# Seven products of quarters for two feature groups instead of one, with three of the four sums of weights made by accumulating DMAs

## The chip, the cores and the metric

The kernel runs on one core of one Trainium2 chip. The metric is device time in microseconds (us). The kernel before took 2288.77 us (median of three runs, 2286.74 to 2290.21).

## The reference

Two transformer layers over 256 tokens of width 2048, in float32. Each layer is a mixer (a gated delta rule with a linear recurrence in the first, two kinds of attention in the second) followed by a gated feed-forward network (FFN) of width 5632. The change touches the two FFNs alone, so only they matter here:

```python
def swiglu(hn, w_gate, w_up, w_down):
    return (jax.nn.silu(hn @ w_gate) * (hn @ w_up)) @ w_down
...
        h = h + swiglu(rmsnorm(h, ffn_norm[layer]), ffn_w_gate[layer], ffn_w_up[layer], ffn_w_down[layer])
```

`hn` is 256 x 2048, `w_gate` and `w_up` are 2048 x 5632, `w_down` is 5632 x 2048.

## The kernel before

**Numbers in two parts.** A float32 operand is split into `hi`, its value rounded to TensorE's fp32r format, and `lo`, the rest. A product is hi·hi + hi·lo + lo·hi, three matmuls. For the weights, ScalarE (ACT) makes `hi` by a copy and VectorE (DVE) makes `lo` by a subtraction: `split`, lines 174 and 175. A load is always a 128 x 1024 tile of 512 KB (`load`, line 168, issued from SyncE's queue, SP). It holds two feature tiles of 128 for 512 output columns, and is called a unit below. `load` rotates over three buffers of `raw`, and in the FFNs every fourth load goes to the extra buffer `raw4`; the hi and lo tiles have four and three buffers (`whi`, `wlo`).

**A block.** `block` computes two products of 512 columns at once (`i` = 0 and 1): gate and up in the first half of an FFN, two column groups of the down projection in the second. The tokens are in two halves of 128 (`t`). Four PSUM banks `F[t][i]` collect the results. The features are in groups `m` of 512, that is four feature tiles, or two units for each `i`. A gate/up block has four groups. The 5632 hidden features are handled in pieces of 4, 4 and 3 groups: a piece makes as many gate/up blocks as it has groups, then two down blocks over those groups. An FFN has 11 gate/up blocks, four down blocks with four groups and two with three.

**A plain group** costs four units. Each unit is multiplied with both token halves: 2 feature tiles x 2 halves x 3 matmuls = 12 matmuls, 48 for the group (`Bank.add`, lines 366 to 368).

**A group by seven products.** Group 0 of each block is treated as a 2 x 2 matrix product of quarters: activations by token half and feature half, weights by feature half and `i` (b11, b12, b21, b22, one unit each). In place of eight quarter products of six matmuls there are seven, 42 matmuls, over sums and differences of quarters. Four combinations of the activation quarters are made once per FFN or piece by `combine` and kept in `comb`. The weights need four sums per block, made by `total` (lines 337, 340, 341): DVE adds two tiles into `T`, ACT copies `T` to `thi`, DVE subtracts to `tlo`. The sums are T1 = b11+b12, T3 = b12+b22, T2 = T1+b22, T4 = T2+b21. Products go to four more banks `M`, or straight into `F`; `ends` (lines 413 to 415) combines the `M` banks into the tiles `e`, which the end of a block adds to `F`.

**Order.** `seven` is a generator that yields after each of its seven products; `block` runs through the plain units `j` and takes steps of `seven` between them. A planner then orders the instructions of each engine. Engines run their own queues in order and wait on each other by semaphores. At the end of a gate/up block DVE adds `F` and `e` into `fa` (L472, L476, L477) and ACT takes the silu (L473); the block after it transposes `fa` into `hid` on TensorE between its plain units (`turn`, L453). At the end of a down block DVE adds `e` and then `F` into `h` (L488, L491).

Of the kernel before, what the change touches and what calls it, by code (L numbers as in the profile page):

```python
# [6 lines left out]
ALU = mybir.AluOpType  # L7
# [4 lines left out]
T = 256  # L12
# [35 lines left out]
def body(tc, A, out):  # L48
# [129 lines left out]
    def unit(src):  # L178

        return split(load(src))  # L180
# [96 lines left out]

    def sumsq(g, *ts):
        for t in ts or range(2):
            j = mx.tile([128, 512], F32, name="junk", tag="t2", bufs=4)  # L280
            S.activation(j, h[:, t, g * 512:(g + 1) * 512], AF.Square, accum_out=ssp[:, t, g:g + 1])

    def to_x(g, w, late=False):
# [47 lines left out]
        return f  # L331


    def total(a, b, name):

        t = mx.tile([128, 1024], F32, name=name, tag="T", bufs=3)
        V.tensor_tensor(out=t, in0=a, in1=b, op=ALU.add)
        hi = mx.tile([128, 1024], F32R, name="thi", tag="thi", bufs=2)
        lo = mx.tile([128, 1024], F32R, name="tlo", tag="tlo", bufs=2)
        S.copy(hi, t)  # L340
        V.tensor_sub(lo, t, hi.bitcast(F32))  # L341
        return t, (hi, lo)

    def combine(x4):

        f = mx.tile([128, 4, T], F32, name="cf", tag="cf", bufs=1)
        c = mx.tile([128, 4, 2, 128], F32, name="cc4", tag="cc4", bufs=1)
        r = mx.tile([128, 2, 4, 2, 128], F32R, name="comb", tag="comb", bufs=2)
        V.tensor_tensor(out=f, in0=x4[:, :, 0].bitcast(F32), in1=x4[:, :, 1].bitcast(F32), op=ALU.add)
        a11, a21, a12, a22 = (f[:, 2 * j:2 * j + 2, t * 128:(t + 1) * 128] for j in range(2) for t in range(2))  # L350
        for i, (x, y) in enumerate(((a21, a22), (a21, a11), (a22, c[:, 1]), (a12, c[:, 2]))):
            V.tensor_tensor(out=c[:, i], in0=x, in1=y, op=ALU.subtract)
# [18 lines left out]
    def block(src, x, comb, nd, hooks, tail=0):  # L371
# [38 lines left out]

        def ends():
# [3 lines left out]
                V.tensor_tensor(out=o, in0=a.t, in1=b, op=op)  # L415
            return [[c1, w5], [v, w7]]

        sevens = [s for m in comb for s in [seven(m)] for _ in range(7)]
        lead, trail = 2, 3 if nd > 3 else 2
        gaps = max(len(plain) - lead - trail, 1)  # L420
        held, e, k = [], None, 0
        for j, (i, u) in enumerate(plain):
            if j in hooks:
                hooks[j]()
            w = unit(src(i, u))
            held.append((i, u, w))
            if j < len(plain) - tail:
                todo, held = [(*held[0], (0, 1))], []
            elif j < len(plain) - 1:
                continue  # L430
            else:
                todo = [(*y, (t,)) for t in range(2) for y in held]
            for i1, u1, w1, tt in todo:
                for t in tt:
                    F[t][i1].add(lambda kk: xs(2 * u1 + kk, t), w1)
            tick()
            while k < len(sevens) and k < (j - lead + 2) * len(sevens) // gaps:
                next(sevens[k])
                k += 1
                if k == len(sevens):  # L440
                    e = ends()
        return [[y.t for y in f] for f in F], e

    def ffn(L, then, fin=None):
# [14 lines left out]
        for piece in (4, 4, 3):  # L459
            hid = ogp.tile([128, 16, 2, T], F32R, name="hid", tag="hid")  # L460
            for j in range(piece):
                hooks = {2: turn, 3: turn} if todo else {}
                if b == 0:
                    hooks[1] = lambda: cx.update({0: combine(X[:, 0:4])})
                    hooks[8] = rstd
                if j == 1:
                    hooks[5] = lambda: ch.update({0: combine(hid[:, 0:4])})
                F, e = block(lambda i, u: gu[b, u, i], lambda k: X[:, k], {0: lambda: cx[0]}, 4, hooks)
                a = [mx.tile([128, 512], F32, name=f"fa{t}", tag="fa", bufs=4) for t in range(2)]
                for t in range(2):  # L470
                    r = nrm["rs"][:, t:t + 1]
                    V.tensor_tensor(out=a[t], in0=F[t][0], in1=e[t][0], op=(ALU.add, ALU.subtract)[t])  # L472
# [698 lines left out]
```

## Time and profile before

| | |
|---|---|
| median of the runs | 2288.77 us (2286.74 to 2290.21) |
| the profiled execution's own time | 2286.04 us |
| its span, first to last instruction | 2284.2 us |
| granted TensorE clock over the span | 0.996 |
| busy share: TensorE (PE), DVE, ACT, GpSimd (POOL) | 99%, 79%, 53%, 0% |
| DMA | 422.35 MB, 185 GB/s on average |

The profile lists busy time by engine, a chain of work followed back from the last instruction, groups of instructions by line with their mean duration, and DMA issues with the time from issue to landing. Matmuls overlap in the records, so their cost is the distance from one start to the next and not the listed duration. The same holds, by about a tenth of a microsecond, for DVE and ACT. A few per cent of the records can be missing.

### The profile page before, as it was taken

The page shows a single profiled execution, that of the slowest core. Times are in us where ns is not written, and L with a number is a line of the kernel's source. Part 1 is how long each engine was busy: PE and PEld are TensorE (multiplying, and loading weights), DVE is VectorE, ACT ScalarE, POOL GpSimd, SP SyncE. Part 2 cuts the span into 40 slices and gives each one's busy share as a digit, 9 for nine tenths or more (in the row PEclk, how much of TensorE's full clock was granted, in tenths as well). Part 3 has the DMA queues.
Part 4 walks back from the last instruction along what each step waited for, and adds up shares of the span by engine and source line. Part 5 has one row for each costly group of instructions (what it writes and reads, how often), then busy time and mean ns, then how long its engine had stood idle before and what let it go on. Part 6 is the DMA issues. An engine that isn't in the chain of part 4 may idle for free.

```text
span 2284.2 us, 31143 instructions
## 1 busy us (share of the span) xinstructions
PE 2259.0 (99%) x11620; PEld 1906.7 (83%) x11620; DVE 1805.0 (79%) x2655; ACT 1205.9 (53%) x1580; POOL 2.0 (0%) x6
## 2 busy tenths in 40 slices
PE   8999999999999999999999999999999999999997
PEld 8999888788888888888878888887888888888886
DVE  6898676688887888888976658857888788787888
ACT  6765654554554554454654444445554455554554
POOL 0000000000000000000000000000000000000000
PEclk9999999999999999999999999999999999999999
DMA  7444445566565566566554455455565565566564
GB/s 244 148 161 155 145 154 181 167 203 201 185 204 202 188 208 192 191 200 201 185 169 166 151 172 168 166 191 179 186 208 194 192 205 197 183 206 204 186 213 147
DMA packets 118647, 422.35 MB, mean 185 GB/s; under 512 B 13248, under 2 KB 14784, under 8 KB 118368
## 3 DMA queue, kind: packets, MB, share of 16 engines
q1 hardware_dynamic: 118208, 419.84, 55.4%
q8 instruction: 91, 1.49, 0.3%
q10 hardware_dynamic: 288, 0.52, 0.1%
q14 instruction: 60, 0.49, 0.1%
HBM read 418.22 MB, written 2.10 MB: 184 GB/s over the span
## 4 chain that ended last, share of the span: by engine, by line
PE 97%; DVE 1%; DMA 1%; ACT 1%; issue 0%; DVEq 0%; ACTq 0%; SPq 0%
PE F L366 17%; PE F L368 17%; PE F L367 17%; PE Pw L194 7%; PE Pw L199 6%; PE Px L268 5%; PE Px L270 4%; PE Px L269 4%; PE M L367 3%; PE M L368 3%; PE M L366 3%; PE Pw L197 2%; PE Pw L198 2%; PE Ph L453 1%; PE Psc L975 1%; DVE wlo L175 0%
## 5 line engine op out<-in xcount | busy, mean ns | idle before, releaser
L174 ACT CAST whi<-raw 128x1024 fp32r<-128x1024 f32 x744 | 779.9, 1052 | 889.1 <-PE F L368 424.1
L175 DVE TENSOR_TENSOR wlo<-raw,whi 128x1024 fp32r<-128x1024 f32 x744 | 906.1, 1222 | 329.5 <-PE F L367 141.9
L366 PE MATMUL F<-whi,X 128*128 128x512 f32 x1100 | 432.2, 393 | 5.6 <-ACT whi L174 5.6
L368 PE MATMUL F<-whi,X 128*128 128x512 f32 x1100 | 429.6, 391 | 0.0
L367 PE MATMUL F<-wlo,X 128*128 128x512 f32 x1100 | 429.4, 390 | 0.0
L199 PE MATMUL Pw<-X,wlo 128*128 128x256 f32 x1104 | 310.2, 281 | 0.0
L366 PEld LDWEIGHTS F<-whi,X 128*128 128x128 f32 x1100 | 206.8, 188 | 48.7 <-ACT whi L174 7.1
L368 PEld LDWEIGHTS F<-whi,X 128*128 128x128 f32 x1100 | 207.2, 188 | 43.6
L367 PEld LDWEIGHTS F<-wlo,X 128*128 128x128 f32 x1100 | 207.5, 189 | 42.1
L194 PE MATMUL Pw<-X,whi 128*128 128x512 f32 x640 | 230.2, 403 | 0.0
L366 PE MATMUL F<-whi,hid 128*128 128x512 f32 x536 | 209.9, 392 | 0.0
L199 PEld LDWEIGHTS Pw<-X,wlo 128*128 128x128 f32 x1104 | 209.5, 190 | 0.2
L368 PE MATMUL F<-whi,hid 128*128 128x512 f32 x536 | 208.7, 389 | 0.0
L367 PE MATMUL F<-wlo,hid 128*128 128x512 f32 x536 | 208.6, 389 | 0.0
L341 DVE TENSOR_TENSOR tlo<-T,thi 128x1024 fp32r<-128x1024 f32 x136 | 165.4, 1221 | 19.8 <-ACT thi L340 19.6
L340 ACT CAST thi<-T 128x1024 fp32r<-128x1024 f32 x136 | 142.7, 1049 | 28.8 <-PE M L368 14.9
L194 PEld LDWEIGHTS Pw<-X,whi 128*128 128x128 f32 x640 | 120.2, 188 | 29.4 <-issue 0.7
L197 PE MATMUL Pw<-X,whi 128*128 128x256 f32 x464 | 135.0, 291 | 0.0
L198 PE MATMUL Pw<-X,whi 128*128 128x256 f32 x464 | 131.4, 283 | 0.0
L368 PEld LDWEIGHTS F<-whi,hid 128*128 128x128 f32 x536 | 100.6, 188 | 21.0
L367 PEld LDWEIGHTS F<-wlo,hid 128*128 128x128 f32 x536 | 100.7, 188 | 20.6
L366 PEld LDWEIGHTS F<-whi,hid 128*128 128x128 f32 x536 | 100.6, 188 | 20.3
(372 smaller groups left out, 3241.9 us busy)
## 6 DMA issues: line engine op xcount, KB each, us to landing
raw<-in_gu SPq DMA_DIRECT2D x352, 512.0 KB, 4.1
raw<-in_dn SPq DMA_DIRECT2D x176, 512.0 KB, 4.2
raw<-in_w0w SPq DMA_DIRECT2D x74, 512.0 KB, 3.6
raw<-in_wo SPq DMA_DIRECT2D x64, 512.0 KB, 3.5
raw<-in_w1w SPq DMA_DIRECT2D x64, 512.0 KB, 3.5
raw<-in_w1x SPq DMA_DIRECT2D x32, 512.0 KB, 3.5
raw<-in_w0x SPq DMA_DIRECT2D x16, 512.0 KB, 3.5
raw<-in_w0w SPq DMA_DIRECT2D x12, 256.0 KB, 5.3
```

The source lines that it names most:

```text
L174: S.copy(hi, raw)
L175: V.tensor_sub(lo, raw, hi.bitcast(F32))
L194: PE.matmul(P.rearrange("p a b -> p (a b)"), hi[:, kk], X[:, k].rearrange("p a b -> p (a b)"), start=k == 0, stop=False)
L197: PE.matmul(P[:, 0], hi[:, kk], X[:, k, 0], start=k == 0, stop=False)
L198: PE.matmul(P[:, 0], hi[:, kk], X[:, k, 1], start=False, stop=False)
L199: PE.matmul(P[:, 0], lo[:, kk], X[:, k, 0], start=False, stop=k == NK - 1)
L268: PE.matmul(Ps[t], x[:, 0, ts], hi[:, kk], start=k == 0, stop=False)
L340: S.copy(hi, t)
L341: V.tensor_sub(lo, t, hi.bitcast(F32))
L366: PE.matmul(self.t, xh, hi[:, kk], start=self.i == kk == 0, stop=False)
L367: PE.matmul(self.t, xh, lo[:, kk], start=False, stop=False)
L368: PE.matmul(self.t, xl, hi[:, kk], start=False, stop=kk == 1 and self.i == self.n - 1)
```

## The change

In each block with four groups, groups 0 and 1 are now both done by seven products and share the four `M` banks; groups 2 and 3 stay plain. In a down block with three groups, group 0 alone is, as before. `combine` accordingly runs for two groups of the FFN's input, and for the first two groups of a piece of four (the first of a piece of three).

The sums of weights are made in another way. b12 is loaded straight into a tile `T0`. T3 is still a DVE addition, of `T0` and b22, into `T1`. The other three sums are made in `T0` in place: GpSimd issues a DMA that reads b11 from memory and adds it to `T0`; once that sum has been split, another that adds b22; and once that has been split, a third that adds b21. b11, b21 and b22 are also loaded as before, because each is needed alone as well. The steps of the two generators are interleaved by a written-out list, and the number of steps taken by each plain unit is a written-out table.

The buffers are rearranged: `T0` has two, `T1` one, `combine` borrows them for its own intermediate tiles, `comb` has four instead of two; in the FFNs `fa` and the scratch tile of `sumsq` have two instead of four.

```diff
-    def total(a, b, name):
-
-        t = mx.tile([128, 1024], F32, name=name, tag="T", bufs=3)
-        V.tensor_tensor(out=t, in0=a, in1=b, op=ALU.add)
+    def halves(t):
+
         hi = mx.tile([128, 1024], F32R, name="thi", tag="thi", bufs=2)
         lo = mx.tile([128, 1024], F32R, name="tlo", tag="tlo", bufs=2)
         S.copy(hi, t)
         V.tensor_sub(lo, t, hi.bitcast(F32))
-        return t, (hi, lo)
+        return hi, lo
...
-        f = mx.tile([128, 4, T], F32, name="cf", tag="cf", bufs=1)
-        c = mx.tile([128, 4, 2, 128], F32, name="cc4", tag="cc4", bufs=1)
-        r = mx.tile([128, 2, 4, 2, 128], F32R, name="comb", tag="comb", bufs=2)
+        f = mx.tile([128, 4, T], F32, name="cf", tag="T1", bufs=1)
+        c = mx.tile([128, 4, 2, 128], F32, name="cc4", tag="T0", bufs=2)
+        r = mx.tile([128, 2, 4, 2, 128], F32R, name="comb", tag="comb", bufs=4)
...
-            b11 = load(src(0, 2 * m))
-            M[0].add(q(0, 0), split(b11))
-            yield
-            b12 = load(src(1, 2 * m))
-            t, w = total(b11, b12, "T1")
-            M[1].add(cx(0), w)
-            yield
+            sums = [mx.tile([128, 1024], F32, name=f"T{i}", tag=f"T{i}", bufs=(2, 1)[i]) for i in range(2)]
+            t = sums[0]
+            more_of = lambda i, u: G.dma_start(t, src(i, 2 * m + u), accum_op=ALU.add)
+            nc.sync.dma_start(t, src(1, 2 * m))
             b22 = load(src(1, 2 * m + 1))
             F[0][1].add(cx(3), split(b22))
             yield
-            M[3].add(cx(1), total(b12, b22, "T3")[1])
-            yield
-            t, w = total(t, b22, "T2")
-            M[2].add(cx(2), w)
-            yield
-            b21 = load(src(0, 2 * m + 1))
-            F[0][0].add(q(1, 0), split(b21))
-            yield
-            F[1][0].add(q(1, 1), total(t, b21, "T4")[1])
+            V.tensor_tensor(out=sums[1], in0=t, in1=b22, op=ALU.add)
+            more_of(0, 0)
+            M[3].add(cx(1), halves(sums[1]))
+            yield
+            M[0].add(q(0, 0), unit(src(0, 2 * m)))
+            yield
+            M[1].add(cx(0), halves(t))
+            more_of(1, 1)
+            yield
+            F[0][0].add(q(1, 0), unit(src(0, 2 * m + 1)))
+            yield
+            M[2].add(cx(2), halves(t))
+            more_of(0, 1)
+            yield
+            F[1][0].add(q(1, 1), halves(t))
             yield
...
-        sevens = [s for m in comb for s in [seven(m)] for _ in range(7)]
-        lead, trail = 2, 3 if nd > 3 else 2
-        gaps = max(len(plain) - lead - trail, 1)
+        two = [seven(m) for m in comb]
+        sevens = [two[i] for i in ((0,) * 7 if ns == 1 else (0, 0, 0, 1, 0, 1, 0, 1, 0, 1, 1, 0, 1, 1))]
+        steps = {2: (0, 4, 8, 12, 13, 13, 13, 14), 1: (0, 2, 4, 6, 7)}[ns]
...
-            while k < len(sevens) and k < (j - lead + 2) * len(sevens) // gaps:
+            while k < len(sevens) and k < steps[min(j, len(steps) - 1)]:
                 next(sevens[k])
                 k += 1
-                if k == len(sevens):
+                if k == len(sevens) - 1:
                     e = ends()
...
-                F, e = block(lambda i, u: gu[b, u, i], lambda k: X[:, k], {0: lambda: cx[0]}, 4, hooks)
-                a = [mx.tile([128, 512], F32, name=f"fa{t}", tag="fa", bufs=4) for t in range(2)]
+                F, e = block(lambda i, u: gu[b, u, i], lambda k: X[:, k], {m: lambda m=m: cx[m] for m in range(2)}, 4, hooks)
+                a = [mx.tile([128, 512], F32, name=f"fa{t}", tag="fa", bufs=2) for t in range(2)]
...
-                F, e = block(lambda i, u: dn[2 * p + i, u0 + u], lambda k: hid[:, k], {0: lambda: ch[0]}, piece,
+                F, e = block(lambda i, u: dn[2 * p + i, u0 + u], lambda k: hid[:, k], {m: lambda m=m: ch[m] for m in range(piece - 2)}, piece,
```

Below, the steps of a group are written as group.step: 0.2 is the second product of group 0. The order over a block with four groups is: plain units 0 and 1; 0.1, 0.2, 0.3, 1.1; plain 2; 0.4, 1.2, 0.5, 1.3; plain 3; 0.6, 1.4, 1.5, 0.7; plain 4; 1.6; plain 5, 6, 7; 1.7. The accumulating DMAs are issued after the addition of step 2 and after the splits of steps 4 and 6, and are needed by the splits of steps 4, 6 and 7 of the same group.

More of the change, by code (lines that the diff above doesn't have):

```diff
@@ L279, in sumsq @@
         for t in ts or range(2):
-            j = mx.tile([128, 512], F32, name="junk", tag="t2", bufs=4)
+            j = mx.tile([128, 512], F32, name="junk", tag="t2", bufs=2 if more else 4)
             S.activation(j, h[:, t, g * 512:(g + 1) * 512], AF.Square, accum_out=ssp[:, t, g:g + 1])
@@ L463, in ffn @@
                 if b == 0:
[L464 to L467, printed above, removed]
-                F, e = block(lambda i, u: gu[b, u, i], lambda k: X[:, k], {0: lambda: cx[0]}, 4, hooks)
-                a = [mx.tile([128, 512], F32, name=f"fa{t}", tag="fa", bufs=4) for t in range(2)]
+                    hooks[1] = lambda: [cx.update({m: combine(X[:, 4 * m:4 * m + 4])}) for m in range(2)]
+                    hooks[5] = rstd
+                if 0 < j <= piece - 2:
+                    hooks[5] = lambda: ch.update({j - 1: combine(hid[:, 4 * j - 4:4 * j])})
+                F, e = block(lambda i, u: gu[b, u, i], lambda k: X[:, k], {m: lambda m=m: cx[m] for m in range(2)}, 4, hooks)
+                a = [mx.tile([128, 512], F32, name=f"fa{t}", tag="fa", bufs=2) for t in range(2)]
                 for t in range(2):
```

## The prediction

> **What bounds the kernel now.** The page comes first: which engine is full, and which the chain of work runs through.
>
> ```profile
> PE 2259.0 (99%) x11620; PEld 1906.7 (83%) x11620; DVE 1805.0 (79%) x2655; ACT 1205.9 (53%) x1580; POOL 2.0 (0%) x6
> ...
> PE 97%; DVE 1%; DMA 1%; ACT 1%; issue 0%; DVEq 0%; ACTq 0%; SPq 0%
> ```
>
> TensorE is busy for the whole span and the chain is TensorE for 97% of it. GpSimd does nothing. Then the busy time by windows, cut at the transposes of three successive gate/up blocks, and the chain in order of time for the pitch inside them.
>
> ```profile
> core 0: us, PE busy (x) PEld busy (x) DVE busy (x) ACT busy (x) POOL busy (x), PEclk, DMA share, GB/s
> 756.36:799.44 43.08, 43.08 (x196) 35.69 (x195) 37.67 (x42) 23.42 (x25) 0.00 (x0) 1.00 0.59 196
> 799.44:842.52 43.08, 43.08 (x196) 35.69 (x195) 34.60 (x36) 22.56 (x25) 0.00 (x0) 1.00 0.58 197
> 842.52:885.60 43.08, 43.08 (x196) 35.69 (x195) 34.69 (x36) 22.55 (x25) 0.00 (x0) 1.00 0.62 193
> ```
>
> ```profile
> 756.36 0.44 PE Ph L453 x4
> ...
> 799.44 0.44 PE Ph L453 x4
> 799.87 0.24 PE F L366
> ...
> 802.61 0.23 PE M L366
> ...
> 803.98 0.44 PE Ph L453 x4
> ```
>
> A gate/up block takes 43.08 us, three times to the hundredth, at full clock and without a gap on PE. It holds 3 x 48 + 42 = 186 matmuls and two sets of transposes of 0.44, so a matmul costs (43.08 - 0.88) / 186 = 0.227 us. The twelve matmuls from 799.87 to 802.61 give 0.228. DVE has 5 to 8 us to spare in a block, ACT 20, and the DMA engines are busy for 0.60 of it. That is the room into which the change moves work.
>
> **TensorE.** A second group by seven saves six matmuls. It comes in 22 gate/up blocks and the 8 down blocks with four groups: 30 x 6 = 180 matmuls, as the built program's order shows (10,589 rows become 10,409). 180 x 0.227 = 40.8 us less on the path, or 1.36 in each of the 30 blocks. The floor of a gate/up block becomes 43.08 - 1.36 = 41.72. PE alone would make 2286.0 - 40.8 = 2245.2.
>
> **DVE and ACT.** Before, a block has 4 sums, 4 remainders of sums and 15 of plain tiles on DVE: 23 operations on 1024 columns. After, it has 2 sums, 8 and 14: 24.
>
> ```profile
> 759.77 1.04 ACT L340 CAST thi<-T 128x1024 fp32r<-128x1024 f32 x1
> ...
> 761.05 1.22 DVE L341 TENSOR_TENSOR tlo<-T,thi 128x1024 fp32r<-128x1024 f32 x1
> 762.18 1.22 DVE L337 TENSOR_TENSOR T<-T,raw 128x1024 f32<-128x1024 f32 x1
> ...
> 764.04 1.23 DVE L349 TENSOR_TENSOR cf<-hid 128x1024 f32<-128x1024 f32 x1
> ...
> 766.31 0.76 DVE L352 TENSOR_TENSOR cc<-cf 128x256 f32<-128x256 f32 x2
> ...
> 790.92 0.69 DVE L472 TENSOR_TENSOR fa<-F,e 128x512 f32<-128x512 f32 x1
> 791.52 0.68 DVE L476 TENSOR_TENSOR e<-F,e 128x512 f32<-128x512 f32 x1
> 792.12 1.22 DVE L337 TENSOR_TENSOR T<-raw 128x1024 f32<-128x1024 f32 x1
> 793.25 0.75 DVE L477 SCALAR_TENSOR_TENSOR fa<-e,rs,fa 128x512 f32<-128x512 f32 x1
> ```
>
> Starts are 1.13 apart (761.05 to 762.18). So DVE gains 1.1 us a block: the mean of the three windows, 35.7, becomes 36.8 of 41.7. ACT gains three copies of 1.04: 22.8 becomes 25.9. Neither is full, and both additions hide beside PE. Six more `combine` runs add about 4 us of DVE each (a `cf` of 1.23, four differences at 0.76 for two, and a remainder as long as `cf`): 25 us in all, hidden in blocks that have 4.9 to spare, but not where DVE waits. The smaller rotation of `fa` costs nothing: the transposes that read it are over by plain unit 3, half a block before it is written again. The scratch of `sumsq` is used only at an FFN's end.
>
> **The accumulating DMAs.** There are 64 groups by seven (44 + 16 + 4), so 192 new transfers of 512 KB from GpSimd, whose queue is empty. No such DMA is in this trace. The nearest rows are loads:
>
> ```profile
> raw<-in_gu SPq DMA_DIRECT2D x352, 512.0 KB, 4.1
> raw<-in_dn SPq DMA_DIRECT2D x176, 512.0 KB, 4.2
> ...
> col<-in_col SPq DMA_DIRECT2D x1, 8.0 KB, 1.7
> ```
>
> ```profile
> DMA to landing us min/median/max: 3.4/4.1/4.8
> ```
>
> A load of this size lands 4.1 us after its issue; 1.7 is there with hardly any data, so 2.4 is the data. Adding to a tile in SBUF reads that tile as well as the memory. Call the time from the end of the DVE operation that releases the DMA to its landing L. Lower bound 3.4 (the fastest load). My value takes the data twice, 1.7 + 4.8 = 6.5, and 1.0 for what it shares the engines with: loads at 0.60 busy, and the other group's accumulation, released about a microsecond later on the same queue. **L = 7.5.** Upper bound: behind one whole doubled transfer, and slower by some, 10.5.
>
> What waits on L? The three sums of a group are made in one tile, one after the other, each only when the one before has been split. A split is an ACT copy, then a DVE subtraction: 759.77 to 761.05 + 1.22 = 762.27, 2.5 us. Count from E, when PE ends a block. The new sum into `T1`, which releases the first DMA, stands on DVE behind the additions that empty `F`, as the sum at 792.12 does now behind 790.92: it ends 793.34 - 790.92 = 2.4 after E. The splits of 0.4, 0.6 and 0.7 are then ready at 2.4 + L + 2.5, 2.4 + 2L + 5.0 and 2.4 + 3L + 7.5. On PE, 0.7 is due after plain units 0 to 3 (4 x 2.72), eleven steps of 1.36 and two transposes: 10.88 + 14.96 + 0.88 = 26.7 after E. Behind 0.7 the block still has 0.7 itself, plain units 4 to 7, 1.6 and 1.7: 10.88 + 4.08 = 14.96. So
>
> period = the larger of 41.7 and 2.4 + 3L + 7.5 + 14.96 = 24.9 + 3L.
>
> 0.6 to 0.7 is the narrow place: three steps, 4.1 us of PE, lie between a split and the next, which need L + 2.5. Group 1 has its sum behind the split of 0.4 (1.2 more) and four times L in line up to 1.7: 2.4 + L + 2.5 + 1.2 + 3L + 7.5 + 1.36 = 15.0 + 4L, later than group 0 only above L = 9.9. The chain shows from L = 5.6 and has eaten the matmuls' gain at (43.08 - 24.9) / 3 = 6.1. With L = 7.5 a block takes 47.4: 4.3 more than now, 129 us over 30 blocks.
>
> Queued behind the waits are, on ACT, the copies of the next weights, on DVE their remainders, in one order with the sums; PE waits for those. On Pool only later accumulations stand behind. On SP the next load of `T0` waits for the last split of the one before, and the loads behind it wait with it.
>
> Two smaller places. The four down blocks with three groups save no matmul, and get the chain: 138 x 0.227 = 31.3 of PE against 2.4 + 3L + 7.5 + 1.36 + 8.16 = 41.9, less some 6 us because the built order puts their first sum before the end of the block ahead. I take 4.5 x 4 = 18 (0 to 42). In down blocks that order also puts the next block's first sum ahead of `ends` on DVE, where it waits for a `T0` load that was itself held by a split; `ends` and the emptying of `F`, which the next block's first matmul needs, come later. A whole load, 4.1, is the most; I take 1.5 for each of 12 blocks, 18 (0 to 49).
>
> **Sum.** 2286.0 (the profiled execution; its span of 2284.2 and 1.8 around it) + 129 + 18 + 18 = 2451; PE's saving is already in the 129. The median of the runs is 2.7 above the profiled execution: 2454. At L = 10.5 a block takes 56.4 (group 1: 57.0): 2730 to 2790 with the smaller places. At L = 3.4 PE is the bound.
>
> **Rivals.** *PE stays the bound (0.25).* If L is below 5.6 the chain hides, and 40.8 less some 6 for the uncovered ends of down blocks is gained: 2254. For it: a load lands in 4.1, an addition on the way may cost little, and a GpSimd queue with nothing else in it releases at once. Against: even at 4.1 the 2.5 of a split makes 6.6, where 4.1 us of PE lie between 0.6 and 0.7, so only the lead gathered earlier covers it, and DVE, in one order, loses that lead at each wait. It decides at L = 6.1 at the latest.
>
> *The DMA engines fill up (0.19).* Now 16 loads take 0.60 x 43.08 = 25.8 us of the engines, 1.61 each. With 16 loads and 6 accumulations at double work, 28 x 1.61 = 45.1: more than the floor of 41.7 even if never idle. At nine tenths busy that is 50.1 us a block, and in full queues L itself grows: at 10, 24.9 + 30 = 54.9, 11.8 more than now, 2286 + 30 x 11.8 + 50 = 2690. At single work 22 x 1.61 = 35.4 fits. The Trainium skill has the rule behind this (Collectives: The Full Stack, "The bandwidth ceiling: the fold count and why AG ≠ RS ≠ AR"): an addition in the DMA engines is not slow as arithmetic, but it reads two sources through one ring, and throughput halves. No run here shows it yet.
>
> That the change doesn't remove the matmuls is excluded by the built order. The forecast, that the chain of three transfers sets the period (L from 6.1 to 9.5), has 0.56; its own range is 2290 to 2650.
>
> **Numbers.** A measurement can tell about 0.2%, 4.6 us, from no change. Faster by more: 0.22, the first rival less its edge. Within: 0.04, L close to 6.1. Slower: 0.74, the rest. The range takes in the first rival and nearly all of the second: 2250 to 2740.
>
> **What would show it.** Gate/up blocks between transposes near 47 us, not 41.7 or 43.1. At least 10 us from GpSimd's issue of one accumulation to the next of the same group (7.5 + 2.5). ACT's `thi` copies waiting for DMAs into `T0`, PE for `thi` and `tlo` with its longest gap before 0.7. A DMA share of 45.1 / 47.4 = 0.95 if the work is double, 0.75 if single. The prediction is wrong if accumulations land in under 5 us, if PE has no gaps, or if the gaps stand elsewhere, such as before plain units behind `raw` loads.

## The result, and the profile after

The changed kernel takes 2577.12 us (median of four runs, 2569.19 to 2586.3) against 2288.45 us beside it: a ratio of 1.1269, 95% interval 1.125 to 1.1289. That is 289 us slower. The prediction said 2454, with a range of 2250 to 2740.

First the page of the changed kernel: engines, granted clock by fortieths of the span, DMA queues, shares of the chain, and DMA issues (last column: us from issue to landing).

```profile
PE 2350.7 (91%) x11440; PEld 1907.2 (74%) x11440; DVE 1840.1 (71%) x2709; ACT 1283.7 (50%) x1676; POOL 167.9 (7%) x198
...
PEclk9999999999999999999899999999999999998999
...
q1 hardware_dynamic: 118208, 419.84, 46.8%
q0 software_dynamic: 27648, 100.68, 22.3%
...
PE 52%; DMA 24%; DVE 13%; issue 9%; ACT 3%; DVEq 0%; POOL 0%; POOLq 0%; ACTq 0%; SPq 0%
...
raw<-in_gu SPq DMA_DIRECT2D x308, 512.0 KB, 5.7
...
T<-in_gu POOLq DMA_DIRECT2D x132, 512.0 KB, 6.2
```

The chain was TensorE for 97% and is now TensorE for 52%, DMA for 24%. No engine is full. The 180 matmuls are gone (x11620 to x11440), yet TensorE's busy time *rose* from 2259.0 to 2350.7: its matmuls take longer, which the clock explains in part (below). The accumulations use the engines heavily: 22.3% x 2576.0 / 192 = 2.99 us of all 16 engines each, against 46.8% x 2576.0 / 800 = 1.51 for a plain load.

By windows, cut at the transposes of successive gate/up blocks as in the prediction (the last one also holds two down blocks):

```profile
825.80:871.60 45.80, 42.88 (x189) 34.24 (x188) 37.49 (x41) 23.95 (x26) 4.32 (x5) 1.00 0.87 250
871.60:924.00 52.40, 45.95 (x189) 35.12 (x188) 39.04 (x42) 25.73 (x28) 5.17 (x6) 0.97 0.78 215
924.00:976.20 52.20, 46.06 (x189) 36.20 (x188) 36.57 (x38) 27.11 (x30) 6.06 (x7) 0.93 0.80 230
976.20:1128.90 152.70, 134.16 (x550) 104.49 (x549) 105.57 (x109) 70.20 (x74) 15.53 (x18) 0.96 0.81 227
```

Sixteen such gate/up blocks average 51.0 us (45.9 to 59.6), where they took 43.1: 16 x 7.9 = 126. Four stretches of one gate/up and two down blocks average 155.0, where they took 127.4: 110. The first blocks of each layer and the pieces of three groups hold the other 53.

The chain in order of time, in the second of these windows (start, duration):

```profile
863.49 1.14 DVE T L395
865.15 8.03 DMA T<-in_gu
...
876.94 9.71 DMA T<-in_gu
...
889.35 7.79 DMA T<-in_gu
...
899.83 5.46 DMA T<-in_gu
907.59 0.68 DVE e L416
...
915.93 1.14 DVE T L395
917.59 9.12 DMA T<-in_gu
```

From one `T1` sum to the next, 52.4 us, the chain is four landings of 8.03, 9.71, 7.79 and 5.46, 31 us in all, with the splits between them. Group 1's accumulations are issued at 876.94, 889.35 and 899.83: 12.4 and 10.5 apart. Who waited for what, over the whole span (us in total, times, longest):

```profile
DVE tlo L339 <- ACT thi L338: 307.1, 128, 7.1
ACT thi L338 <- DMA T<-in_gu: 275.6, 98, 8.1
...
ACT thi L338 <- DMA T<-in_dn: 116.4, 40, 5.5
```

ACT stands at the head of its queue for a landing, and DVE behind ACT.

### The profile page after: what moved, and what is told of

The parts are those of the page before. It is cut to its first block, busy times and chain, and to the rows that moved or that the text cites. A ratio compares the mean times of both kernels' runs of the same rounds, so it can differ in the third digit from the quotient of the medians.

```text
span 2576.0 us, 31617 instructions
## 1 busy us (share of the span) xinstructions
PE 2350.7 (91%) x11440; PEld 1907.2 (74%) x11440; DVE 1840.1 (71%) x2709; ACT 1283.7 (50%) x1676; POOL 167.9 (7%) x198
## 3 DMA queue, kind: packets, MB, share of 16 engines
q1 hardware_dynamic: 118208, 419.84, 46.8%
q0 software_dynamic: 27648, 100.68, 22.3%
## 4 chain that ended last, share of the span: by engine, by line
PE 52%; DMA 24%; DVE 13%; issue 9%; ACT 3%; DVEq 0%; POOL 0%; POOLq 0%; ACTq 0%; SPq 0%
DMA T<-in_gu 14%; PE Pw L194 6%; PE F L365 5%; PE F L364 5%; PE Pw L199 5%; DMA T<-in_dn 5%; PE F L366 5%; PE Px L268 4%; PE Px L270 4%; PE Px L269 4%; DVE wlo L175 3%; DVE tlo L339 3%; DVE e L416 2%; DMA raw<-in_dn 2%; PE Pw L197 2%
## 5 line engine op out<-in xcount | busy, mean ns | idle before, releaser
L175 DVE TENSOR_TENSOR wlo<-raw,whi 128x1024 fp32r<-128x1024 f32 x714 | 861.0, 1218 | 242.2 <-ACT whi L174 75.1
L339 DVE TENSOR_TENSOR tlo<-T,thi 128x1024 fp32r<-128x1024 f32 x256 | 312.2, 1220 | 308.0 <-ACT thi L338 307.1
L338 ACT CAST thi<-T 128x1024 fp32r<-128x1024 f32 x256 | 268.1, 1049 | 449.6 <-DMA T<-in_gu 275.6
L364 PE MATMUL F<-whi,X 128*128 128x512 f32 x792 | 326.6, 413 | 31.3 <-DVE fa L473 12.9
L365 PE MATMUL F<-wlo,X 128*128 128x512 f32 x792 | 320.1, 404 | 4.2 <-DVE wlo L175 4.1
L366 PE MATMUL F<-whi,X 128*128 128x512 f32 x792 | 317.8, 401 | 0.0
L390 POOL DMA_DIRECT2D T<-in_gu x132 | 114.1, 864 | 1870.2 <-DMA raw<-in_gu 886.5
L364 PEld LDWEIGHTS F<-whi,X 128*128 128x128 f32 x792 | 154.8, 196 | 81.5 <-DVE h L492 13.7
L364 PE MATMUL F<-whi,hid 128*128 128x512 f32 x424 | 176.6, 418 | 30.1 <-DVE h L492 15.2
L365 PE MATMUL M<-tlo,comb 128*128 128x512 f32 x384 | 161.0, 419 | 37.2 <-DVE tlo L339 37.0
L364 PE MATMUL M<-thi,comb 128*128 128x512 f32 x384 | 159.9, 416 | 30.9 <-ACT thi L338 19.0
L366 PEld LDWEIGHTS F<-whi,X 128*128 128x128 f32 x792 | 155.1, 196 | 33.9
L366 PE MATMUL F<-whi,hid 128*128 128x512 f32 x424 | 170.9, 403 | 0.0
L366 PE MATMUL M<-thi,comb 128*128 128x512 f32 x384 | 155.5, 405 | 0.0
L395 DVE TENSOR_TENSOR T<-T,raw 128x1024 f32<-128x1024 f32 x64 | 78.0, 1218 | 81.6 <-DMA raw<-in_dn 49.2
```

Of the source, the lines that this page charges most:

```text
L175: V.tensor_sub(lo, raw, hi.bitcast(F32))
L364: PE.matmul(self.t, xh, hi[:, kk], start=self.i == kk == 0, stop=False)
L365: PE.matmul(self.t, xh, lo[:, kk], start=False, stop=False)
L366: PE.matmul(self.t, xl, hi[:, kk], start=False, stop=kk == 1 and self.i == self.n - 1)
L390: more_of = lambda i, u: G.dma_start(t, src(i, 2 * m + u), accum_op=ALU.add)
```

## The experiments

Each kernel is compared with the kernel before, run beside it (2286 to 2288 us). Those that differ from the changed kernel by a line or two show that edit against it.

### Taking the addition out of the transfers

```diff
-            more_of = lambda i, u: G.dma_start(t, src(i, 2 * m + u), accum_op=ALU.add)
+            more_of = lambda i, u: G.dma_start(t, src(i, 2 * m + u))
```

> The 192 GpSimd transfers are left as they are in number, size, order and waits, but they overwrite the tile and do not add to it (the sums of weights are left out, so the numbers computed are others). Theory A (the chain of three transfers and the queues behind it set the period, and adding doubles a transfer's work): the transfers land about 2 us sooner, about 6 us in place of 8, and with three in line 6 us of the 9 lost per block come back: 2280 to 2350 us. Theory B (the DMA engines are full): their work falls from 16 x 1.44 + 6 x 2.97 = 41 us to 32 us a block, PE is the bound: 2250 to 2270 us. Theory C (GpSimd's way of issuing is what is slow, not the addition): no change, 2540 to 2590 us.

This kernel leaves the three sums out, since a transfer now overwrites its tile. It took 2406.8 us (2405.14 to 2409.41), ratio 1.0526 [1.0511, 1.0542]. Its queue of transfers and their landings:

```profile
q0 software_dynamic: 27648, 100.68, 12.6%
...
T<-in_gu POOLq DMA_DIRECT2D x132, 512.0 KB, 5.2
```

So 170 us of the 290 come with the addition: the same bytes in the same chain use 12.6% x 2407.6 / 192 = 1.58 us of the engines in place of 2.99, land 1.0 us sooner in gate/up blocks, and GpSimd's issue takes 0.53 us in place of 0.86. Another 120 us stay without it. The time lies between the ranges of A (up to 2350) and C (from 2540), and none of the three theories had it.

### Two landings in line in place of three

The same number of accumulations, but b11 is added both to `T0` and to `T1`, and b21 to `T1`, so that two transfers of a group run side by side. `T1` also gets a second buffer, for which the scratch tile of `sumsq` moves into the buffers of `fa`; this is not in the lines shown.

```diff
-            more_of(0, 0)
+            more_of(0, 0, t)
             M[3].add(cx(1), halves(sums[1]))
+            more_of(0, 0, sums[1])
...
             M[1].add(cx(0), halves(t))
-            more_of(1, 1)
...
-            M[2].add(cx(2), halves(t))
-            more_of(0, 1)
+            M[2].add(cx(2), halves(sums[1]))
+            more_of(0, 1, sums[1])
...
-            F[1][0].add(q(1, 1), halves(t))
+            F[1][0].add(q(1, 1), halves(sums[1]))
```

> The same sums with the same number and size of accumulating DMAs, but only two of them in line: b11 is added to T0 for the sum b11+b12 and, by another transfer, to T1 (which holds b12+b22) for the second sum; b21 is then added to T1. Theory A (chain): about one landing, 8 us, leaves the line of each group; the group's later waits take part of it back: 2400 to 2490 us. Theory B (DMA engines full, 41 us of work a block as before): no change, 2550 to 2600 us.

2537.16 us (2534.29 to 2540.04), ratio 1.11 [1.1081, 1.1118]: 40 us back, no more, and between the two ranges. A third of the chain is gone, but the landings that are left got slower:

```profile
T<-in_gu POOLq DMA_DIRECT2D x132, 512.0 KB, 8.1
```

8.1 us in place of 6.2. The number of landings in line and the time of one are not independent: transfers side by side share the engines. Theory A, which held L fixed, falls in its size. What the second buffer gives by itself was not run.

### One group in place of two

```diff
-                F, e = block(..., {m: lambda m=m: cx[m] for m in range(2)}, 4, hooks)
+                F, e = block(..., {0: lambda: cx[0]}, 4, hooks)
```

(and group 0 alone in down blocks)

> Only group 0 of each block by seven products, as in the kernel before (no matmul saved), with its sums by accumulating DMAs. The DMA work is 16 x 1.44 + 3 x 2.97 = 32 us of a 43 us block. Theory A (chain): the line of three landings is still there, and 0.7 comes at plain unit 4 in a block of twelve: 5 to 9 us a block over the kernel before, 2400 to 2520 us. Theory B (engines full): room enough, 2280 to 2300 us. Theory D (the second group is what the other queues cannot carry): 2280 to 2300 us.

2525.07 us (2520.76 to 2530.1), ratio 1.1043 [1.1023, 1.1064], just outside A's range and far from the others'. With half the accumulations (12.4% of the engines) and before's number of matmuls it is still 238 us slower than before. A crowd on the DMA engines is not needed for the loss; the chain of one group is enough, in the places that the table gives it. Those are narrow: with one group, all seven steps are over by plain unit 4 of twelve, where the kernel before spreads them up to plain unit 7. One group with its steps spread was not run, so how the 238 us divide between the landings and the places stays open.

### All sums by DVE, in the change's order and in turn

Both groups, all loads plain, each sum a DVE addition as in the kernel before:

```diff
+            t, w = total(b11, b12, "T1")
+            M[1].add(cx(0), w)
...
+            M[3].add(cx(1), total(b12, b22, "T3")[1])
...
+            t, w = total(t, b22, "T2")
...
+            F[1][0].add(q(1, 1), total(t, b21, "T4")[1])
```

> Two groups by seven with the order and the table of steps of the change, but all four sums by DVE additions as in the kernel before (order of the products inside a group as before; no accumulating DMA). DVE then has 30 operations of 1024 columns a block, about 41.3 us by start distances against PE's 41.7. Theories A and B (the accumulating DMAs are the loss): nearly all comes back, but DVE leaves no slack: 2290 to 2350 us. Theory D (the second group itself): 2450 us or more.

2389.12 us (2386.02 to 2392.74), ratio 1.0449 [1.0433, 1.0464]: between the ranges. Two stretches of 45 us from its first layer:

```profile
600.00:645.00 45.00, 42.92 (x186) 33.38 (x185) 41.26 (x42) 26.26 (x29) 0.00 (x0) 1.00 0.59 190
645.00:690.00 45.00, 42.09 (x180) 32.36 (x179) 42.15 (x44) 22.36 (x24) 0.00 (x0) 1.00 0.53 167
```

DVE works 41 to 42 us of 45, TensorE 42 to 43: my reading is that neither has room for the other's bursts. The same sums with one group after the other in even places:

```diff
-        sevens = [two[i] for i in (... (0, 0, 0, 1, 0, 1, 0, 1, 0, 1, 1, 0, 1, 1))]
-        steps = {2: (0, 4, 8, 12, 13, 13, 13, 14), 1: (0, 2, 4, 6, 7)}[ns]
+        sevens = [two[i] for i in (... (0, 0, 0, 0, 0, 0, 0, 1, 1, 1, 1, 1, 1, 1))]
+        steps = {2: (0, 2, 4, 6, 8, 10, 12, 14), 1: (0, 2, 4, 6, 7)}[ns]
```

> Edit: against the kernel with both groups' sums on DVE (2389 us): the same additions, but one group after the other in even places, as the kernel before has its single group. Theory D1 (DVE itself is full with 42 to 43 us of a 45 us block, so the order matters little): 2350 to 2395. Theory D2 (the order of the two groups made DVE's bursts): 2270 to 2330.

2384.41 us (2383.21 to 2385.41), ratio 1.0423 [1.0407, 1.0438]: D1. Between these two orders there are 5 us; the order of the steps is not what costs here.

### Three sums by GpSimd

```diff
+        (E or V).tensor_tensor(out=t, in0=a, in1=b, op=ALU.add)
...
+            t, w = total(b11, b12, "T1", G)
...
+            t, w = total(t, b22, "T2", G)
...
+            F[1][0].add(q(1, 1), total(t, b21, "T4", G)[1])
```

> Edit: both groups by seven products stay, but one group follows the other as in the kernel before, all quarters are plain loads, and the sums T1, T2, T4 are additions by GpSimd in SBUF, T3 one by DVE; no transfer adds. Theory A (what costs is the accumulating transfer, in its chain and in the engines' work; GpSimd has room for 64 x 3 additions beside all else): time 2260 to 2300, at or a little below the kernel before, DVE about as busy as there. Theory D (GpSimd and DVE get in each other's way when both work in SBUF, or a GpSimd addition takes over 4 us): 2320 to 2480, seen as DVE's splits longer than in the kernel before or as waits for POOL. Theory E (seven products of quarters cost time in whatever way the sums come): over 2400.

2535.94 us (2530.46 to 2536.68), ratio 1.1086 [1.107, 1.1103]: beyond D's range. It is inside E's (over 2400), but E's reason, that two groups cost as much however their sums come, doesn't fit the 2384 of the same order with DVE sums. Groups by line (busy, mean ns):

```profile
L175 DVE TENSOR_TENSOR wlo<-raw,whi 128x1024 fp32r<-128x1024 f32 x714 | 1041.1, 1470 | 169.4 <-PE Px L269 63.7
...
L337 POOL TENSOR_TENSOR T<-T,raw 128x1024 f32<-128x1024 f32 x128 | 384.3, 3002 | 573.0 <-DMA raw<-in_gu 299.0
...
L341 DVE TENSOR_TENSOR tlo<-T,thi 128x1024 fp32r<-128x1024 f32 x256 | 372.6, 1462 | 53.9 <-ACT thi L340 53.6
```

A GpSimd addition takes 3.0 us, and while it runs DVE's splits are held up: 1041.1 + 372.6 against 861.0 + 312.2 for the same operations in the changed kernel, 240 us for 192 additions, 1.25 each. The delay falls on few of them: 847 of the 970 subtractions still take 1.2 us, and 123 take more than 1.4, up to 3.5, about a whole GpSimd addition. DVE's additions that read one operand from PSUM (`e`, 0.68) are no longer beside a GpSimd addition than elsewhere. A sum on GpSimd costs DVE as much as making it on DVE (1.22), and is later. The Trainium skill (GPSIMD Engine Reference, "1. Specifications") says that GpSimd's SBUF interfaces are shared with VectorE, with contention for instructions that have two SBUF inputs; the subtractions of the splits are such, and the rows agree.

### No sums at all

The kernel with DVE sums in the change's order, with the additions left out (the second quarter is split again where the sum was).

> Edit: the kernel of the change's order and table with all quarters as plain loads, and the additions of quarters left out: where a sum of two quarters stood, the second of the two is split once more. (That part of the computation is changed: the sums.) Same products, same splits, same number of loads. It shows what is left for the products alone. Theory A (the 180 products that go are worth 41 us, and the change's order costs nothing by itself; what costs is how the sums are made): 2240 to 2262. Theory E (the order, its narrow places and the second combination cost in any case): 2280 to 2350. Clock falls none or few.

2327.04 us (2322.7 to 2332.81), ratio 1.0174 [1.0156, 1.0192]: E. Even with no sum made in any way, two groups by seven are 40 us slower than one, not 41 faster. TensorE isn't full:

```profile
548.80:592.40 43.60, 42.40 (x189) 34.34 (x188) 36.81 (x41) 25.90 (x29) 0.00 (x0) 1.00 0.62 189
592.40:636.80 44.40, 42.40 (x189) 34.33 (x188) 34.46 (x36) 24.96 (x28) 0.00 (x0) 1.00 0.62 192
```

It waits, and the longest wait in the waits view is ACT's for plain loads. The first row is this kernel, the second the kernel before:

```profile
ACT whi L174 <- DMA raw<-in_gu: 243.8, 151, 5.7
```

```profile
ACT whi L174 <- DMA raw<-in_gu: 86.1, 60, 3.6
```

The loads land as fast as before (4.1 us), so they are issued late. Quarters that are needed for two splits hold their `raw` buffers longer, two groups at a time, and the loads behind them wait. ACT also waits for TensorE to free one of the two `thi` tiles (93.1 us in 53 places). These two fit the waits; a kernel with more buffers, or without sums in the even places, was not run, so the cause of these 81 us (40 + 41) is argued, not shown.

### One accumulation a group

T1, T3 and T2 by DVE; only b21 into T4 is an accumulating transfer. The lines are against the kernel with DVE sums in turn. The places differ from it as well: group 0's last step comes after three steps of group 1, and the table is (0, 3, 5, 7, 9, 12, 13, 14).

```diff
-            b21 = load(src(0, 2 * m + 1))
-            F[0][0].add(q(1, 0), split(b21))
+            G.dma_start(t, src(0, 2 * m + 1), accum_op=ALU.add)
+            F[0][0].add(q(1, 0), unit(src(0, 2 * m + 1)))
             yield
-            F[1][0].add(q(1, 1), total(t, b21, "T4")[1])
...
+            S.copy(hi, t)
+            V.tensor_sub(lo, t, hi.bitcast(F32))
+            F[1][0].add(q(1, 1), (hi, lo))
```

> Edit: two groups, one after the other with an overlap of one step; T1, T3, T2 by DVE, and of the accumulating transfers only the last, b21 into T4, is left: one per group instead of three, 64 instead of 192, its landing two steps ahead of its use. Theory A (three landings in line are the cost, one has room): 2270 to 2320. Theory B (each accumulation costs engine time and slows the loads beside it): a third of the 190 us that separate the change from sums on DVE, 2400 to 2460. Theory D (DVE, 2 x 3 additions): 2330 to 2390.

2551.59 us (2545.96 to 2552.33), ratio 1.1148 [1.1132, 1.1165]. All three theories missed: with one accumulation a group, 8.0% of the engines, the kernel is hardly faster than with three, and 167 us slower than with all sums on DVE. The timeline at the end of a block shows one such landing:

```profile
594.08 0.86 POOL L405 DMA_DIRECT2D T<-in_gu  x1 [24.20 <-DVE tlo L341]
603.00 1.04 ACT L410 CAST thi<-T 128x1024 fp32r<-128x1024 f32 x1 [6.91 <-DMA T<-in_gu]
...
604.10 0.80 PE L366 MATMUL F<-thi,X 128*128 128x512 f32 x1 [5.42 <-ACT thi L410]
```

Group 1's only accumulation is issued at 594.08, when its T2 has been split, and ahead of its last step only the products of T2, those of b21 and the last plain units are left. ACT stands 6.91 us for the landing, TensorE 5.42. A single landing in line costs most of its length here, where little is left to put beside it, and in ACT's queue the next block's splits stand behind it. By this row, what counts is not how many landings a block has but how much of them stands uncovered. The changed places may have a part in the 167 us too: no run has them with all sums on DVE.

### The places of the steps, and a third buffer for the sums

```diff
-        steps = {2: (0, 4, 8, 12, 13, 13, 13, 14), 1: (0, 2, 4, 6, 7)}[ns]
+        steps = {2: (0, 3, 5, 7, 9, 11, 13, 14), 1: (0, 2, 4, 6, 7)}[ns]
```

> Edit: only the table of the places of group 1's steps between those of group 0, from (0, 4, 8, 12, 13, 13, 13, 14) to (0, 3, 5, 7, 9, 11, 13, 14); the same transfers, sums and products. Theory A (a block's length is set by the chain of landings of each group, laid end to end with the narrow places of the table, among them the three steps 1.3, 1.4, 1.5 behind one step of group 0): with the places even, blocks without down work come from 47 to about 44 to 45, time 2400 to 2480. Theory B (the transfers crowd the DMA engines, the order matters little): 2550 to 2590. Theory C (the order of the table was the better one, the even one makes group 0 late): over 2590.

2531.83 us (2523.24 to 2539.34), ratio 1.1071 [1.1039, 1.1102]: 45 us back, between A and B. TensorE's gaps gather in one place, the last step 1.7, and the sixteen gate/up blocks average 49.7 (45.1 to 54.5) in place of 51.0.

The third buffer, again in the changed kernel's places (to make room, the scratch tile of `sumsq` moves into the buffers of `fa`):

```diff
-            sums = [... bufs=(2, 1)[i]) for i in range(2)]
+            sums = [... bufs=(3, 1)[i]) for i in range(2)]
```

> Edit: three buffers instead of two for the sum that the transfers add to, at the price of a scratch buffer shared with the row products; the order and the transfers are the same. Theory A (the load of b12 into a sum's buffer waits for the last split of the group two before, and holds SP's queue and DVE's first sum behind it, above all in down blocks): that wait, 132.9 us in 50 places on SP's queue, is gone, time 2530 to 2560. Theory B (the load is early enough anyway and the chain starts later than it): 2570 to 2585. Theory C (the earlier load collides with the accumulating transfers): 2585 to 2620.

2557.18 us (2553.39 to 2566.25), ratio 1.119 [1.1167, 1.1213]: 20 us back, in A's range, though the wait that A named is hardly shorter. SP's queue, changed kernel first:

```profile
SPq L168 <- DVE T L395: 140.2, 40, 8.3
SPq L391 <- DVE tlo L339: 132.9, 50, 4.7
```

```profile
SPq L391 <- DVE tlo L339: 120.7, 48, 5.0
...
SPq L168 <- DVE T L395: 35.0, 32, 2.2
```

The load of `T0` (L391) still waits 120.7 us; what fell is the wait of ordinary loads behind DVE's first sum (L395), from 140.2 to 35.0.

### The granted clock

In the changed kernel the clock falls to half after TensorE has been half idle. The timeline of TensorE ahead of one such fall, with only the matmuls that waited (in brackets how long, and for what), then windows across it:

```profile
927.83 0.50 PE L364 MATMUL M<-thi,comb 128*128 128x512 f32 x1 [0.46 <-ACT thi L338]
929.09 0.50 PE L365 MATMUL M<-tlo,comb 128*128 128x512 f32 x1 [0.76 <-DVE tlo L339]
...
931.36 0.49 PE L364 MATMUL M<-thi,comb 128*128 128x512 f32 x1 [0.85 <-ACT thi L338]
934.23 0.79 PE L365 MATMUL M<-tlo,comb 128*128 128x512 f32 x1 [2.37 <-DVE tlo L339]
```

```profile
926.18:929.59 3.41, 2.20 (x9) 1.30 (x8) 1.78 (x2) 2.86 (x3) 0.26 (x1) 1.00 0.12 47
929.59:933.00 3.41, 1.41 (x5) 0.59 (x4) 3.41 (x5) 2.56 (x4) 1.46 (x2) 1.00 0.63 98
933.00:936.42 3.42, 2.19 (x5) 1.81 (x6) 2.31 (x3) 0.11 (x1) 0.00 (x0) 0.50 0.99 258
936.42:939.83 3.41, 3.41 (x9) 2.64 (x9) 1.22 (x1) 1.88 (x2) 0.00 (x0) 0.50 1.02 292
939.83:943.24 3.41, 3.41 (x18) 2.80 (x18) 1.82 (x2) 2.90 (x5) 1.17 (x2) 1.00 1.06 338
```

The granted clock (third column from the end) goes to 0.50 at 933.0, 1.1 us into the longest of four short gaps, and back at 939.8. In the fourth window TensorE is busy throughout and has 9 matmuls where the fifth has 18. In windows of 2 us the 760 us of the first layer from 500 on show 14 such falls; the clock that is missing adds up to 35.9 us at full speed. Over the whole span it is 2576.0 x (1 - 0.963) = 95, against 2284.2 x (1 - 0.996) = 9 in the kernel before, which has no fall in those 760 us.

The Trainium skill (TensorE: Matmul & The Clock Gate, "What's actually happening") says that the clock drops to half after an idle window of about 3.4 us. The trace shows the window, but not that it has to be idle. From 400 us on, the changed kernel's profile has 36 falls. They start whole multiples of 3.413 us apart, and the windows above are cut there; each lasts one, two or three such windows. In the window ahead of a fall TensorE was never busy for more than 0.53 of it (1.41 of 3.41 us in the second row), and of the 538 windows at full clock that no fall followed none was under 0.48. In 34 of the 36 no single gap had reached 3.4 us when the clock fell: several short gaps in one window were enough. The profiles of the kernel before and of seven experiments divide in the same place, between 0.44 and 0.57.

Two kernels put products of zeros, added into a sum that they leave as it is, where TensorE waits: twelve ahead of 0.7 in the changed kernel, and twenty ahead of 1.7 in the kernel with even places.

```diff
+            if m == 0 and ns > 1:
+                for _ in range(12):
+                    PE.matmul(M[2].t[:, 0:128], tb["mz"], tb["mz"], start=False, stop=False)
             F[1][0].add(q(1, 1), halves(t))
```

> Edit: twelve TensorE products of zeros, added into a sum that they don't change, right ahead of the eighth step of group 0 (0.7) in each gate and up block with two groups; nothing else moves. In the trace of the changed kernel the granted clock falls to about 0.53 for some 6 us thirteen times in the first layer (34 us of full-clock work), each time after TensorE stood at the waits ahead of 0.7. Theory G (the clock is lowered because of these gaps, and what it slows lies on the path): fewer of these falls, under 6 in the first layer, mean clock up from 0.963 to 0.975 or more, time 2520 to 2570 although work is added. Theory H (the clock costs nothing, since TensorE waits for the landings anyway): the number of falls may drop, time 2570 to 2585. Theory J (the gaps are not what lowers it, or the products fill TensorE itself): falls as before, time 2577 to 2640 (30 blocks by up to 2 us).

2601.14 us (2595.6 to 2605.01), ratio 1.1375 [1.1354, 1.1395]: 24 us slower and in J's range, with 12 falls of 20.4 us in the first layer in place of 14 of 35.9. The fillers took 85 us (24 records of TensorE in a block, 2.8 us, and not the 0.13 each that I had assumed), and the gaps came back at other steps. It doesn't settle the question.

> Edit: the even table of places (2532 us by itself), and twenty TensorE products of zeros of about 0.13 us each, added into a sum that they don't change, right ahead of the last step of group 1 (1.7), where TensorE waits 3.2 and then 2.1 us in each block and the granted clock falls to 0.50 for some 6.5 us right after (15 falls and 51 us of full-clock work in the first layer). Theory G (the falls lie on the path): 4 falls or fewer in the first layer and 2440 to 2500. Theory H (TensorE only waits longer at the next landing when it is not slowed): falls go, clock up from 0.956, time 2515 to 2540. Theory J (the products are in the way): 2545 to 2590.

2514.28 us (2512.49 to 2515.56), ratio 1.0988 [1.097, 1.1006]. The place, in windows, without and with the fillers:

```profile
896.00:900.00 4.00, 0.73 (x2) 0.30 (x2) 1.72 (x2) 1.43 (x2) 0.00 (x0) 0.92 0.93 373
900.00:904.00 4.00, 2.71 (x6) 2.15 (x7) 4.00 (x6) 1.61 (x2) 0.86 (x1) 0.50 0.64 98
```

```profile
896.00:900.00 4.00, 4.00 (x31) 3.72 (x30) 1.47 (x2) 0.50 (x1) 0.00 (x0) 1.00 1.03 275
900.00:904.00 4.00, 2.95 (x23) 2.56 (x22) 3.57 (x5) 2.54 (x3) 0.86 (x1) 1.00 0.70 246
```

The falls are nearly gone (3 in the first layer in place of 15, 6.8 us in place of 51), and with 139 us of TensorE work added the kernel is 18 us *faster*. So the falls do follow from the gaps, and some 18 us of what they slow lay on the path of this kernel. The mean clock went from 0.956 to 0.985, some 74 us over the span, so most of the clock that came back was waited away at the next landing, as H said; the time lies 14 us above G's range and 0.7 below H's. The part that the falls have in the changed kernel's 289 us stays open: at most 95 - 9 = 86, an estimate, and the fillers there brought no gain.

No kernel here beats the kernel before; the nearest is the one that leaves the sums out.

## Why the prediction was right, and where it was off

**The bound moves from TensorE to a chain of landings: right.** The chain of work, the waits and the one-group kernel show it. The mechanism given 0.56 came about, with a time 123 us above its number: the loss is 289 us where 165 were forecast.

**TensorE saves 40.8: the matmuls go, the time doesn't.** x11620 became x11440. But the kernel without sums is 81 us above what the matmuls alone would give. The step that took PE's floor, 41.7, as the larger of two terms had no term for splits, buffers and order that are late without any chain.

**DVE and ACT: busy times right in kind, not harmless.** DVE gained 35 us over the span, neither engine filled. "Hidden in blocks that have 4.9 to spare" is true of the sum and not of the order: the kernels with DVE sums, at 41 to 42 of 45 us, are some 100 us slower than before.

**L = 7.5: right on average, but not one number.** The view of the accumulating line has, from issue to landing:

```profile
DMA to landing us min/median/max: 5.1/6.0/11.1
```

L starts earlier, mostly by 0.3 us, at the end of the DVE operation that releases the transfer. Counted so over the 192 accumulations it is 7.4 us on average (median 6.3), and 7.5 in gate/up blocks. The work doubled as the term 2 x 2.4 assumed (2.99 against 1.51 us of the engines). But the lengths differ: in gate/up blocks the first accumulation of group 1, issued 0.9 to 3.2 us behind the second of group 0, takes 10.2 on average and the one after it 7.9, the others 6 to 8. I had also not counted that the plain loads slow down, from 4.1 to 5.7.

**Which line is the longer: the other one.** The chain above runs through group 0's first landing and then group 1's three. That is the prediction's second line, 15.0 + 4L, which it set aside below L = 9.9 because it gave every landing the same length. From their release the four are 8.55, 10.00, 8.08 and 5.75, 32.4 in all, and the line gives 47.4; group 0's own three (8.55, 5.94, 5.81) give 45.2 by 24.9 + 3L. The block took 52.4.

**The end of the block: the term that was too small.** The missing 5 us stand between the last split and the sum that releases the next chain. DVE, and TensorE's last product of the block:

```profile
906.45 1.23 DVE L339 TENSOR_TENSOR tlo<-T,thi 128x1024 fp32r<-128x1024 f32 x1 [1.70 <-ACT thi L338]
...
910.15 0.39 PE L366 MATMUL F<-thi,X 128*128 128x512 f32 x1
...
910.52 0.68 DVE L473 TENSOR_TENSOR fa<-F,e 128x512 f32<-128x512 f32 x1
...
914.65 0.68 DVE L473 TENSOR_TENSOR fa<-F,e 128x512 f32<-128x512 f32 x1
...
915.85 1.21 DVE L395 TENSOR_TENSOR T<-T,raw 128x1024 f32<-128x1024 f32 x1
```

From the split's end, 907.68, to the sum's end, 917.06, it is 9.4 us, and so it is in all ten places where the second or third gate/up block of a piece is followed by another; the prediction had 1.36 + 2.4 = 3.8. (At the ends of the other blocks the order puts the sum ahead of that split.) The 2.4 itself came back, from 914.65 to 917.06, but it doesn't begin where TensorE ends. `ends`, three splits of the next block and the additions of the first token half come first. The prediction had read 790.92 as the end of TensorE's block; counted back from the transposes at 799.27 by the 30 products ahead of them, that block ended at 792.5, and its sum 0.9 after it.

**Down blocks: under-sized.** Forecast were 4.3 for each with four groups, 18 in all for the four with three, and 18 in all, 1.5 each, for the first sum ahead of `ends`. A gate/up block with two down blocks of four groups grew by 27.6; taking 7.9 for the first leaves 10 for each down block, where 5.8 were forecast. The third buffer for `T0`, which takes most of the wait behind the first sum away, gave back 20 in all.

**The narrow place 0.6 to 0.7: half.** In the first layer (500 to 1260 us) TensorE's idle time ahead of steps with `thi` or `tlo` into `F` (0.7, 1.7) adds up to 27 us, the steps into `M` (0.4, 1.2, 0.6, 1.4, 1.6) to another 27, the beginnings of blocks to 24. The two longest gaps (4.9 and 4.5 us) are ahead of such a step into `F`.

**The rival of full DMA engines: its work, not its effect.** The engines' share in the windows is 0.78 to 0.87, not 0.95: the work doubled but never filled them. The rule of the Trainium skill named there (two sources through one ring, half the throughput) agrees: 1.99 times the engine time per MB of the plain loads, 22.3% for 100.68 MB against 46.8% for 419.84, and 1.89 times that of the same transfers without the addition (2.99 against 1.58 us). What it did was lengthen L and the loads: without the addition 170 us come back.

**Missed altogether: the clock.** The prediction counted TensorE's waits but not that TensorE is slower after them.

In sum, taken off one after the other (a different order would share them out differently): 2577 with everything; 2407 without the addition; 2327 without sums, chain or queue; 2246 by the matmuls alone. So 170 is the addition, 80 the chain of transfers that would remain, 81 what two groups cost in this order without any sum, against 41 gained. Only the first of these is a difference of one line; the kernel without sums also has another order of products inside a group, other buffers and fewer DVE additions, and 2246 is worked out, not run.

## What to carry to other kernels

A transfer that an engine's in-order queue must wait for costs what of it stands uncovered, in every place where it is in line; the kernel with one such transfer a group, placed at the end of a block, was hardly faster than the one with three. When a chain's start hangs on an engine that also ends the block before, count its whole queue from there to the release and not only the operation itself. Before moving work to an idle engine or to the DMA engines, look for what it shares with the busy ones: here both the DMA addition and the GpSimd addition took back what they were to save. Where a change opens gaps on TensorE, price the slower clock too: here it followed wherever TensorE was busy for less than about half of a window of 3.41 us.

## What the runs showed of the hardware that was not expected

- An accumulating transfer of 512 KB into SBUF takes 2.99 us of the 16 engines against 1.58 for the same transfer without the addition, and 0.86 us of GpSimd to issue against 0.53.
- A GpSimd addition of 128 x 1024 takes 3.0 us and costs DVE 1.25 us of delay on average, as much as DVE would need for it; it falls on 123 of 970 subtractions of two SBUF operands, which take up to 3.5 us in place of 1.2.
- An accumulating transfer issued 0.9 to 3.2 us behind another took 10.2 us from its release in the gate/up blocks, against 7.4 for all 192.
- The granted clock halves for one to three fixed windows of 3.413 us after a window in which TensorE was busy for about half or less (at most 0.53 ahead of all 36 falls, at least 0.48 where none followed), also by several short gaps; filling the gaps with products of zeros made a kernel faster by 18 us with 139 us of added work.
